# An encoder block on one core: the conditioning vector first, its later sums on two engines, and four changes of order

## The chip, the cores and the metric

The kernel runs as one program on one core of a Trainium2 chip. The core has TensorE (PE, matrix products; PEld is its loading of stationary operands), VectorE (DVE), ScalarE (ACT), GpSimd (POOL) and SyncE (SP), each with its own queue in program order, and 16 DMA engines that they share. SBUF holds the tiles, PSUM (eight banks of 128 x 512 float32) takes TensorE's results. The metric is the device time of one execution in microseconds; where several were run, their median.

## The reference, cut to what matters

One layer, 256 tokens of width 1024, all in float32. The conditioning vector c (1024) gives six modulation vectors of 1024 each: silu(c) times a matrix of 1024 x 6144, plus a bias.

```
mod = silu(c) @ w_ada + b_ada                       # 6 x 1024
h   = rmsnorm(x, g_pre_mix) * (1 + scale_m) + shift_m
proj = h @ w_in                                     # 5664 columns: q, k, v, z, xbc, dt
attn = mixture over 3 dilated windows (16 heads of 64, ALiBi)
y    = two-way SSD scan of conv5(xbc), dt = softplus(..), gated by silu(z), rmsnorm
x    = x + gate_m * rmsnorm(concat(attn, y) @ w_out, g_post_mix)
h   = rmsnorm(x, g_pre_ffn) * (1 + scale_f) + shift_f
logits = h @ w_router + b_router                    # top 4 of 32 experts, softmax over the 4
ffn = sum over experts e of weight_e * (swiglu(h @ w_gate_up[e] + b) @ w_down[e] + b)
x    = x + gate_f * rmsnorm(ffn, g_post_ffn)
```

All 32 experts' weights (12 MB each) are read. An expert gets only the tokens that chose it, gathered by a product with a selection matrix; up to 64 fit into the first pass, and a branch per expert (`more`) takes further passes where there are more.

## The kernel before, in words

**The ring of weights.** Every large weight comes through one list `loads` of tiles of 128 x 2048 float32 (1 MB). `consumed` (L133) marks tiles as used and issues the next loads on SyncE (L150), in list order, into whatever slots are free. The ring has 7 slots at first (`RING`); `more_ring` adds 3, 3, 2, 3 and 3 more as the mixer's pools close, 21 in the end. The list: eight chunks of w_ada for shift and scale of the mixer (`W_ADA`, 128 rows x 2048 columns each), then the 22 tiles of w_in (256 columns each) with 16 tiles of w_ada for the other four vectors (`W_MOD`) between them from the seventh on, then eight of w_out, then twelve for each expert (eight of gate and up, four of down). A DMA signals its landing on one of a few semaphores, taken in turn; a DMA whose semaphore is still owed by an earlier one waits in its queue. x, the small vectors, the identity and conv_w are issued on ScalarE's queue instead (L246 to L257), in program order with ScalarE's own work.

**Head.** The small vectors land as rows of one tile `vec` and are transposed into columns `colv` (L289, L290); silu of the first eight columns gives `csT`. x is squared and scaled into `xn` and transposed into four PSUM banks (L371). `ada_sums` (L330) multiplies each chunk by csT as stationary operand, four column groups side by side; `ada` transposes the result into columns `modT`. Then, for each of eight blocks of 128 channels, ScalarE writes the modulated block (L443), and it is cut into a rounded high part `hh` and the rest `hl`.

**Projections.** A float32 product is done as three products of high and low parts (`mm3`, L386). The weights are cut half a tile at a time by `split`: ScalarE makes the high part (L377), VectorE the low part (L378); `ahead` issues that two halves before their use, with three buffers. For each of the 22 tiles n and half h, `unit` issues 48 or 24 products, then `mod_half` (L355) the products of a quarter of the modulation: tile i = n - 5, two of its four blocks of rows, four column groups each, accumulated in PSUM; `cs31` holds column k of csT in the middle of zeros, so that group g's sum lands in its own row. `evac` takes results out, in pieces.

**Background pieces.** `bg` (L315) issues the next piece of a list of generators: `cumulate`, `ssd_bg`, then `att_bg` (L696). It is called in the middle of a unit and after it, as often as `PACE` says (four times a tile from n = 14 on). `att_bg` issues, for head pair j, when `ready` says that its keys are there: scores with VectorE's minimum and ScalarE's exponentials (`att_scores`), a piece; the scaling of pair j-1 (`att_norm`, L664); once the values are there, the product with the values of pair j-2, a piece; the transposes of pair j-1 (`att_T`, L678), a piece. `softplus_dt` (L469) is a chain on 128 x 64 elements in two pieces: the addition of the bias (L472), transposes on TensorE (L475) and exponentials at n = 1, first half; twenty small VectorE operations at n = 1, second half.

**Experts.** After the router, `rank` and `cnt` (the experts' counts) are made; `count(0)` (L1052) loads a count into a register of TensorE, ScalarE and VectorE, `hint` (L1055) tells each engine's branch prefetcher what the count makes of the branch; eight gathers follow (L1040, L1043), the softmax of the routing weights `comb` (L1066 to L1072), and the loop over experts, which begins with the branch (L1223). For the last expert the work goes in halves; `down_piece` (L1312) accumulates both column halves in one PSUM bank (partitions 0 to 63 and 64 to 127), which VectorE (L1338) and ScalarE (L1339) then copy out.

## Time and profile before

| | us |
|---|---|
| median of three runs | 1299.23 (1298.46 to 1304.69) |
| profiled execution: its own time, its span | 1302.06, 1300.0 |
| TensorE busy | 1166.8 (90%) |
| VectorE busy | 360.4 (28%) |
| ScalarE busy | 279.8 (22%) |
| GpSimd busy | 23.7 (2%) |
| DMA | 465.99 MB, mean 358 GB/s |
| mean granted clock of TensorE | 0.981 |

The strips of the page, 40 slices of 32.5 us each; a digit is the share in tenths, PEclk the granted clock in tenths of full speed:

```
PE   3799989988899999999989999999999999999986
PEld 1788867766333333333353333333333334333332
DVE  0686664457221111112211121111111121111112
ACT  1576556654111000001110011000000011100001
PEclk9899999999799999999999999999999899999998
DMA  8877655486699999999999999999999999999995
GB/s 312 259 250 258 207 184 178 157 315 263 268 415 414 412 415 412 416 413 415 415 405 406 413 415 413 414 414 414 415 415 404 415 410 415 404 413 408 416 345 205
```

The mixer fills the first ten slices, the experts the rest. Shares of busy time are means over these two stages with different limits. Where a row gives an idle time in brackets, the arrow names what ended it. In the table by stretches a number of instructions follows each engine's busy time.

### The profile page before, as it was taken

To read this page: it belongs to the slowest core of one execution; us is meant where nothing else is said; L and a number is where in the kernel's file an instruction comes from. 1 tells how busy PE (TensorE), PEld (TensorE's weight loads), DVE (VectorE), ACT (ScalarE), POOL (GpSimd) and SP (SyncE) were. 2 spreads that over 40 slices of the span, in tenths; PEclk is the share of its full clock that TensorE was granted. 3 is DMA by queue.
4 is the path that set the end of the run, shared out by engine and by line. 5 is a ranking of instruction groups with operands and counts; after the bars stand their busy time and mean duration, and the time that the engine had idled before them with its cause. 6 is when DMAs were issued, how large, how long until landed. Compare 5 with 4: busy or idle time off the path is not lost. (4 is left out here: it accounts for less than half of the span.)

```text
span 1300.0 us, 17236 instructions
## 1 busy us (share of the span) xinstructions
PE 1166.8 (90%) x6901; PEld 586.7 (45%) x6901; DVE 360.4 (28%) x768; ACT 279.8 (22%) x619; POOL 23.7 (2%) x34
## 2 busy tenths in 40 slices
PE   3799989988899999999989999999989999999986
PEld 1788867766333333333353333333333334333332
DVE  0686664457221111112211121111111121111112
ACT  1576556654111000001110011000000011100001
POOL 0100010010000000000000000000000000000000
PEclk9899999999799999999999999999999899999998
DMA  8877655486699999999999999999999999999995
GB/s 312 259 250 258 207 184 178 157 315 263 268 415 414 412 415 412 416 413 415 415 405 406 413 415 413 414 414 414 415 415 404 415 410 415 404 413 408 416 345 205
DMA packets 115645, 465.99 MB, mean 358 GB/s; under 512 B 11083, under 2 KB 34291, under 8 KB 82707
## 3 DMA queue, kind: packets, MB, share of 16 engines
q1 hardware_dynamic: 114752, 462.39, 90.2%
q8 instruction: 107, 1.75, 0.6%
q10 hardware_dynamic: 723, 1.33, 0.3%
q14 instruction: 63, 0.52, 0.1%
HBM read 462.65 MB, written 1.05 MB: 357 GB/s over the span
## 5 line engine op out<-in xcount | busy, mean ns | idle before, releaser
L1128 PE MATMUL pq_g<-w,xg 128*64 128x512 f32 x992 | 263.2, 598 | 2.8 <-DMA w<-in_w_gate_up_dram 2.8
L1128 PE MATMUL pq_u<-w,xg 128*64 128x512 f32 x992 | 263.2, 596 | 1.3 <-issue 1.3
L1166 PE MATMUL pq_u<-w,aT 128*64 128x512 f32 x992 | 219.7, 595 | 2.1
L1140 ACT ACTIVATE sg<-g 128x512 f32<-128x512 f32 (+1 forms) x32 | 19.9, 623 | 689.5 <-DVE g L1139 689.5
L1139 DVE TENSOR_SCALAR g<-pq_g 128x512 f32<-128x512 f32 (+1 forms) x32 | 21.9, 683 | 449.5 <-PE pq_g L1128 254.3
L1128 PEld LDWEIGHTS pq_u<-w,xg 128*64 128x64 f32 x992 | 75.0, 138 | 137.3 <-issue 135.2
L1128 PEld LDWEIGHTS pq_g<-w,xg 128*64 128x64 f32 x992 | 74.2, 138 | 130.3 <-issue 110.6
L1166 PEld LDWEIGHTS pq_u<-w,aT 128*64 128x64 f32 x992 | 68.5, 137 | 131.6 <-issue 120.2
L386 PE MATMUL ps_pj<-hh,wh 128*128 128x256 f32 x296 | 89.7, 303 | 3.4 <-DVE hh L444 3.4
L378 DVE TENSOR_TENSOR wl<-w,wh 128x1024 fp32r<-128x1024 f32 x60 | 74.7, 1246 | 58.7 <-ACT wh L377 58.6
L386 PE MATMUL ps_pj<-hh,wl 128*128 128x256 f32 x296 | 85.4, 288 | 2.3 <-DVE wl L378 2.3
L386 PE MATMUL ps_pj<-hl,wh 128*128 128x256 f32 x296 | 85.3, 288 | 0.0
L1230 DVE COPY y<-pq_u 128x512 f32<-128x512 f32 x31 | 21.4, 692 | 227.8 <-PE pq_u L1166 227.4
L1040 PEld LDWEIGHTS pq_m<-sel,xt 128*128 128x128 f32 x544 | 67.1, 201 | 26.3 <-issue 25.6
L1040 PE MATMUL pq_m<-sel,xt 128*128 128x128 f32 (+1 forms) x544 | 73.1, 291 | 1.2 <-DVE top L1066 1.2
L1043 ACT ACTIVATE xg<-pq_m,modT,g 128x128 f32<-128x128 f32 x128 | 48.3, 458 | 110.5 <-PE pq_m L1040 110.5
L377 ACT ACTIVATE wh<-w 128x1024 fp32r<-128x1024 f32 x60 | 63.5, 1058 | 28.7 <-PE ps_t L386 10.9
L386 PEld LDWEIGHTS ps_pj<-hh,wh 128*128 128x128 f32 x296 | 58.1, 196 | 9.3 <-issue 9.0
L1177 PE MATMUL o<-y,sT 64*128 64x512 f32 x248 | 61.6, 615 | 0.0
L386 PEld LDWEIGHTS ps_pj<-hh,wl 128*128 128x128 f32 x296 | 57.9, 196 | 2.8 <-DVE wl L378 2.7
L386 PEld LDWEIGHTS ps_pj<-hl,wh 128*128 128x128 f32 x296 | 58.0, 196 | 0.1
L1095 PE MATMUL pq_m<-kc,selw 128*128 128x128 f32 x66 | 16.3, 315 | 29.0 <-DVE selw L1091 28.2
(316 smaller groups left out, 1032.9 us busy)
## 6 DMA issues: line engine op xcount, KB each, us to landing
w<-in_w_gate_up_dram SPq DMA_DIRECT2D x248, 1024.0 KB, 19.2
w<-in_w_down_dram SPq DMA_DIRECT2D x127, 1024.0 KB, 20.0
w<-in_w_ada_dram SPq DMA_DIRECT2D x24, 1024.0 KB, 5.2
w<-in_w_in_dram SPq DMA_DIRECT2D x22, 1024.0 KB, 13.3
w<-in_w_out_dram SPq DMA_DIRECT2D x8, 1024.0 KB, 4.8
w<-in_w_gate_up_dram SPq DMA_DIRECT2D x16, 512.0 KB, 15.2
xt<-in_x_dram ACTq DMA_DIRECT2D x1, 1024.0 KB
w<-in_w_down_dram SPq DMA_DIRECT2D x2, 512.0 KB
```

Of the source, the lines that this page charges most:

```text
L377: act.activation(hi.bitcast(F32R), src, AF.Copy)
L378: dve.tensor_sub(lo.bitcast(F32R), src, hi)
L386: pe.matmul(out_ap, u, v, start=first and i == 0, stop=last and i == 2, skip_group_check=True)
L1040: pe.matmul(p[:, w * i:w * i + w], res[:, t, k * 128:(k + 1) * 128], sel[:, t], start=(t == 0), stop=(t == 1))
L1043: act.activation(xg[:, k], p[:, w * i:w * i + w], AF.Identity, bias=m_shift[:, k:k + 1], scale=g1[:, 8 + k:9 + k])
L1095: pe.transpose(p[:, 128 * t:128 * t + 128], selw[:, t].rearrange("p d c -> p (d c)"), ident)
L1128: pe.matmul(dst[cs * q:cs * q + cs, 0:w], xg[:, k], weight(k, o, w), start=False, stop=(k == KD - 1), tile_position=(0, cs * q), skip_grou ...
L1139: dve.tensor_scalar(g, pg, 7.0, None, op0=OP.min)
L1140: act.activation(s, g, AF.Sigmoid, scale=1.702)
L1166: pe.matmul(py[cs * q:cs * q + cs, 0:w], a4[:, k % nj, k // nj, :], weight(KD + k, w * q, w), start=(k == 0), stop=(k == KD - 1), tile_pos ...
L1177: pe.matmul(oacc[t][hf], sT[64 * q:64 * q + 64, 128 * t:128 * t + 128], y[64 * q:64 * q + 64, :], start=False, stop=False, tile_position=( ...
L1230: dve.tensor_copy(y, py)
```

## The change

The parts, in program order. (1) `c` is the first DMA on ScalarE's queue, then the identity, then x. Its eight columns are transposed and put through silu by themselves; the seven other vectors and conv_w are issued after silu. The squares and the scaling of x are emitted after the second chunk of `ada_sums`, the transposes of the other vectors (`columns`) and of x (`tokens_T`) after the sixth. (2) `mod_half`: of the two tiles of a group g, the first (rows 0 to 511 of w_ada) is multiplied and summed on VectorE into `macc` (one scaling, three multiply-adds of 128 x 512), the second stays on TensorE; `macc` is then summed over its partitions on TensorE with a column of ones (`one31`), four products more. (3) The first tile's split goes behind the first block of h; high parts of odd blocks are made on ScalarE, all low parts on VectorE. (4) `softplus_dt` has one piece more: the transposes come at n = 1, second half, the small operations at n = 2. (5) `att_bg` issues the scaling of pair j-1 ahead of the scores of pair j, and keys or values count as ready only two background steps after their copy. (6) The first branch's hint is a fixed one, emitted before the counts are made; the count is loaded after the gathers; two products on a bank nobody reads follow the clearing of the output banks. (7) The last expert's result goes into two banks, one for each column half, and the transposes of its second half are emitted ahead of all down products.

```diff
@@ -238,23 +238,29 @@
...
     dtc = mi.tile([32, 1], F32, name="dtc")
     arow = mi.tile([P, 32], F32, name="arow")
-    cs31 = mi.tile([P, KD, 63], F32, name="cs31")
+    one31 = mi.tile([P, 63], F32, name="one31")
+    pool.memset(one31, 0.0)
+    pool.memset(one31[:, 31:32], 1.0)
+    cs31 = mi.tile([P, 4, 63], F32, name="cs31")
     pool.memset(cs31, 0.0)
     dsk = mx.tile([P, 8], F32, name="dsk")
     wdt = cvb[:, 1, :].rearrange("p (k n) -> p k n", k=KD)
-    act.dma_start(xt, x[0].rearrange("(t p) d -> p t d", p=P))
     vo = {}
+    def vec_in(r, half, *items):
+        for nm, src, n in items:
+            act.dma_start(vec[r:r + n, half, :], src.rearrange("(n q) -> n q", q=128))
+            r += n
     r = 0
-    dve.memset(vec, 0.0)
-    for nm, src, n in (("c", c[0], 8), ("gpm", g_pre_mix[0], 8), ("bada", b_ada[0], 48),
-                       ("gpf", g_pre_ffn[0], 8), ("cb", conv_b[0], 12), ("gsn", g_ssd_norm[0], 8),
-                       ("gqm", g_post_mix[0], 8), ("gqf", g_post_ffn[0], 8)):
-        act.dma_start(vec[r:r + n, 0, :], src.rearrange("(n q) -> n q", q=128))
+    for nm, n in (("c", 8), ("gpm", 8), ("bada", 48), ("gpf", 8), ("cb", 12), ("gsn", 8), ("gqm", 8), ("gqf", 8)):
         vo[nm] = r
         r += n
+    vec_in(0, 0, ("c", c[0], 8))
     act.dma_start(ident, keep[:, 0:P])
-    act.dma_start(vec[0:60, 1, :], conv_w[0].rearrange("t (n q) -> (t n) q", q=128))
+    act.dma_start(xt, x[0].rearrange("(t p) d -> p t d", p=P))
     kb_f = flat_v[:, 1536:1536 + sum(KEEPB.values())]
     def loads_dt():
@@ -278,24 +284,37 @@
     def col(nm, j):
         return colv[:, vo[nm] + j:vo[nm] + j + 1]
-    for t in range(2):
-        act.activation(vt[:, t, :], xt[:, t, :], AF.Square, accum_out=tiny[:, t:t + 1])
-    for t in range(2):
-        rstd_of(tiny[:, 2 + t:3 + t], tiny[:, t:t + 1])
     xn = xtk
-    for t in range(2):
-        dve.tensor_scalar(xn[:, t, :], xt[:, t, :], tiny[:, 2 + t:3 + t], None, op0=OP.mult)
     pv = ps("t", 2)
-    pe.transpose(pv[:, 0:128], vec[:, 0, :], ident)
-    pe.transpose(pv[:, 128:188], vec[0:60, 1, :], ident[0:60, 0:60])
-    dve.tensor_copy(colv[:, 0:108], pv[:, 0:108])
-    dve.tensor_copy(colv[:, 108:168], pv[:, 128:188])
-    ghalf = mx.tile([P, KD], F32, name="ghalf")
-    dve.tensor_scalar(ghalf, colv[:, vo["gsn"]:vo["gsn"] + 8], 0.5, None, op0=OP.mult)
+    pe.transpose(pv[:, 64:72], vec[0:8, 0, :], ident[0:8, 0:8])
+    dve.tensor_copy(colv[:, 0:8], pv[:, 64:72])
     csT = mx.tile([P, KD], F32, name="csT")
     act.activation(csT, colv[:, 0:8], AF.Silu)
-    dve.tensor_copy(cs31[:, :, 31:32], csT[:, :, None])
-    dve.tensor_copy(ident_b, ident)
+    vec_in(8, 0, ("gpm", g_pre_mix[0], 8), ("bada", b_ada[0], 48))
+    act.dma_start(vec[0:60, 1, :], conv_w[0].rearrange("t (n q) -> (t n) q", q=128))
+    vec_in(60, 1, ("gpf", g_pre_ffn[0], 8), ("cb", conv_b[0], 12), ("gsn", g_ssd_norm[0], 8),
+           ("gqm", g_post_mix[0], 8), ("gqf", g_post_ffn[0], 8))
+    def tokens_in():
+        dve.tensor_copy(cs31[:, :, 31:32], csT[:, 4:8, None])
+        for t in range(2):
+            act.activation(vt[:, t, :], xt[:, t, :], AF.Square, accum_out=tiny[:, t:t + 1])
+        for t in range(2):
+            rstd_of(tiny[:, 2 + t:3 + t], tiny[:, t:t + 1])
+        for t in range(2):
+            dve.tensor_scalar(xn[:, t, :], xt[:, t, :], tiny[:, 2 + t:3 + t], None, op0=OP.mult)
+    ghalf = mx.tile([P, KD], F32, name="ghalf")
+    def columns():
+        pe.transpose(pv[:, 0:64], vec[0:64, 0, :], ident[0:64, 0:64])
+        dve.tensor_copy(colv[:, 8:64], pv[:, 8:64])
+        pe.transpose(pv[:, 128:232], vec[0:104, 1, :], ident[0:104, 0:104])
+        dve.tensor_copy(colv[:, 64:108], pv[:, 188:232])
+        dve.tensor_copy(colv[:, 108:168], pv[:, 128:188])
+        dve.tensor_scalar(ghalf, colv[:, vo["gsn"]:vo["gsn"] + 8], 0.5, None, op0=OP.mult)
+        dve.tensor_copy(ident_b, ident)
     def bias_parts(pl):
@@ -311,9 +330,11 @@
     pssq = mp.tile([P, 512], F32, name="pssq", tag="ssq", bufs=1)
     bg_list = []
+    ticks = [0]
     def bg(n=1):
         for _ in range(n):
+            ticks[0] += 1
             while bg_list:
                 try:
...
@@ -337,8 +358,12 @@
...
             if k == 1:
                 loads_dt()
+                tokens_in()
             if k == 3:
                 loads_cum()
+            if k == 5:
+                columns()
+                tokens_T()
         loads_late()
         return pa
@@ -352,23 +377,42 @@
                        pt.rearrange("p (j q r) -> p q j r", j=4, q=4)[:, :, :, 0],
                        colv[:, vo["bada"]:vo["bada"] + 16].rearrange("p (q j) -> p q j", q=4))
+    def mod_sums(g, lhs, w, first=False):
+        for b in range(4):
+            pe.matmul(pssq[32 * b:32 * b + 32, 128:256], lhs, w[:, 128 * b:128 * b + 128],
+                      start=first, stop=True, tile_position=(0, 32 * b), skip_group_check=True)
     def mod_half(i, a):
         w = wt[W_MOD[i]].rearrange("p (k n) -> p k n", k=4)
         g = i // 2
+        if i % 2 == 0 and a == 0:
+            macc[g] = mb.tile([P, 512], F32, name="macc", tag="macc", bufs=1)
         for kk in range(2 * a, 2 * a + 2):
-            k = 4 * (i % 2) + kk
-            for b in range(4):
-                pe.matmul(pssq[32 * b:32 * b + 32, 128:256], cs31[:, k, 31 - g:63 - g], w[:, kk, 128 * b:128 * b + 128],
-                          start=(i == 0 and k == 0), stop=True, tile_position=(0, 32 * b), skip_group_check=True)
+            if i % 2:
+                if kk == 2:
+                    mod_sums(g, one31[:, 31 - g:63 - g], macc.pop(g))
+                mod_sums(g, cs31[:, kk, 31 - g:63 - g], w[:, kk, :], kk == 0 and g == 0)
+            elif kk == 0:
+                dve.tensor_scalar(macc[g], w[:, kk, :], csT[:, 0:1], None, op0=OP.mult)
+            else:
+                dve.scalar_tensor_tensor(macc[g], w[:, kk, :], csT[:, kk:kk + 1], macc[g], op0=OP.mult, op1=OP.add)
         if a:
             consumed(W_MOD[i] + 1)
-    ptx = [ps("bc", 2), ps("bc", 2), ps("pj", 3), ps("pj", 3)]
-    for k in range(KD):
-        for t in range(2):
-            o = (k % 2) * 256 + t * 128
-            pe.transpose(ptx[k // 2][:, o:o + 128], xn[:, t, k * 128:(k + 1) * 128], ident)
+    macc = {}
+    ptx = []
+    def tokens_T():
+        ptx.extend([ps("bc", 2), ps("bc", 2), ps("pj", 3), ps("pj", 3)])
+        for k in range(KD):
+            for t in range(2):
+                o = (k % 2) * 256 + t * 128
+                pe.transpose(ptx[k // 2][:, o:o + 128], xn[:, t, k * 128:(k + 1) * 128], ident)
     def split(i, a, pl=None, bufs=3):
@@ -436,13 +480,17 @@
...
     dve.scalar_tensor_tensor(g1[:, 0:8], modT[:, 8:16], 1.0, colv[:, vo["gpm"]:vo["gpm"] + 8],
                              op0=OP.add, op1=OP.mult)
-    ahead(0)
     for k in range(KD):
         src = ptx[k // 2][:, (k % 2) * 256:(k % 2) * 256 + 256]
         full = big("hfull")[:, 0:S]
         act.activation(full, src, AF.Identity, bias=modT[:, k:k + 1], scale=g1[:, k:k + 1])
-        dve.tensor_copy(hh[:, k, :], full)
-        (pool if k % 2 else dve).tensor_sub(hl[:, k, :], full, hh_[:, k, :])
+        if k % 2:
+            act.activation(hh[:, k, :], full, AF.Copy)
+        else:
+            dve.tensor_copy(hh[:, k, :], full)
+        dve.tensor_sub(hl[:, k, :], full, hh_[:, k, :])
+        if k == 0:
+            ahead(0)
     ahead(1)
@@ -470,6 +518,7 @@
         ut = flat_v[0:32, 0:S]
         dve.tensor_scalar(ut, pdt[0:32, 0:S], dtc, None, op0=OP.add)
+        yield
         pt = ps("t", 2)
         for t in range(2):
...
@@ -664,7 +713,11 @@
                 act.activation(sc[:, t, :], sc[:, t, :], AF.Copy, scale=st[:, 6 + t:7 + t])
     prTs, done_in = {}, []
-    ready = {"k": 0, "v": 0}
+    ready = {"k": [], "v": []}
+    def is_ready(what, i):
+        return len(ready[what]) > i and ticks[0] > ready[what][i] + 1
     def att_T(j):
         pr = pts.pop(j)
@@ -695,15 +748,15 @@
     def att_bg():
         for j in range(HEADS // 2 + 2):
+            if 0 < j < 9:
+                att_norm(j - 1)
             if j < 8:
-                while ready["k"] <= j // 2:
+                while not is_ready("k", j // 2):
                     yield
                 att_scores(j)
                 yield
-            if 0 < j < 9:
-                att_norm(j - 1)
             if j > 1:
-                while ready["v"] <= (j - 2) // 2:
+                while not is_ready("v", (j - 2) // 2):
                     yield
                 att_out(j - 2)
...
@@ -736,13 +789,13 @@
...
             act.activation(vt[:, :, c0 - 2048:c0 - 1792], v3, AF.Copy)
             yield
-            ready["v"] += 1
+            ready["v"].append(ticks[0])
         elif c0 >= 1024:
             j = (c0 - 1024) // 128
...
                 kT[j + i] = blk("k")
                 act.activation(kT[j + i], v3[:, i], AF.Copy)
-            ready["k"] += 1
+            ready["k"].append(ticks[0])
             yield
         else:
...
@@ -776,7 +829,7 @@
...
                 chain = softplus_dt(pdt)
                 next(chain)
-            if n == 1 and h:
+            if (n, h) in ((1, 1), (2, 0)):
                 next(chain, None)
             pace = PACE[0 if n < 8 else 1 if n < 14 else 2][2 * h:]
...
@@ -1002,6 +1055,8 @@
         return mq.tile([P, 512], F32, name="pq_" + tag, tag=tag, bufs=bufs)
+    tc.mark_branch_hint_location("more0", hint="LikelyTaken", engines=[ET.PE, ET.Activation, ET.DVE])
     rank = mo.tile([P, 2, NE], F32, name="rank")
     cnt = mo.tile([1, NE], I32, name="cnt")
...
@@ -1019,6 +1074,7 @@
...
     pe.matmul(pcn, ones_b, mask_b[:, 1, :], start=False, stop=True)
     clear(1)
+    keep_warm(pq("u", 1), 2)
     dve.scalar_tensor_tensor(rank, mask, -FAR, prk[:, 0:2, :], op0=OP.mult, op1=OP.add)
     dve.tensor_copy(cnt, pcn[0:1])
@@ -1054,10 +1110,9 @@
     def hint(e, n):
         tc.mark_branch_hint_location(f"more{e}", hint=(n > C), engines=engines)
-    n = count(0)
-    hint(0, n)
     for ks in HALF:
         gather(sel_n, xgs[0], ks)
+    n = count(0)
     comb = mo.tile([P, 2, NE], F32, name="comb")
@@ -1313,7 +1368,7 @@
...
             o = 256 * f + 128 * (k % 2) + C * (k % 4 // 2)
             for q in range(2):
-                pe.matmul(py[C * q:C * q + C, :], aT[:, o:o + C], weight(KD + k, 512 * q, 512),
+                pe.matmul(py[q][C * q:C * q + C, :], aT[:, o:o + C], weight(KD + k, 512 * q, 512),
                           start=(k == 0), stop=(k == KD - 1), tile_position=(0, C * q), skip_group_check=True)
     gate_up_half(0, range(KD))
@@ -1323,10 +1378,9 @@
...
     gate_up_half(1, range(4, KD))
     glu_half(1)
-    py = pq("m", 2)
-    down_piece(0, (0, 1))
+    py = pq("g", 1), pq("u", 1)
     turn_half(1)
-    down_piece(0, (2, 3))
+    down_piece(0, range(4))
     down_piece(1, range(4))
@@ -1335,8 +1389,8 @@
     fo = [[spare[0][:, 1024 * t + 512 * i:1024 * t + 512 * i + 512] for i in range(2)] for t in range(2)]
     y2 = mo.tile([P, 512], F32, name="y2", tag="g")
-    dve.tensor_copy(y[0:C], py[0:C])
-    act.activation(y2[C:P], py[C:P], AF.Copy)
+    dve.tensor_copy(y[0:C], py[0][0:C])
+    act.activation(y2[C:P], py[1][C:P], AF.Copy)
     rsf = []
     for t in range(2):
```

## Rows read from the trace of the kernel before

**Rows 1.** Stretches: length; busy PE, PEld, DVE, ACT, POOL; clock; DMA share; GB/s
```profile
346.00:1278.00 932.00, 861.59 (x4410) 344.10 (x4406) 155.87 (x324) 93.57 (x238) 1.90 (x1) 0.99 1.01 409
340.51:347.34 6.83, 5.36 (x16) 1.80 (x18) 1.74 (x9) 1.56 (x2) 0.00 (x0) 0.50 0.01 4
```

**Rows 2.** SyncE's timeline from 318 us: start, length, engine, line, operation, count
```profile
328.74 18.14 SPq L150 DMA_DIRECT2D w<-in_w_down_dram  x2
```

**Rows 3.** The table by stretches, two stretches of the projections
```profile
84.00:100.00 16.00, 15.59 (x178) 13.76 (x174) 15.41 (x31) 10.29 (x18) 0.00 (x0) 1.00 0.78 248
100.00:181.00 81.00, 80.56 (x872) 69.50 (x870) 53.45 (x88) 49.97 (x107) 6.71 (x7) 1.00 0.69 225
```

**Rows 4.** The timeline of the start; in brackets idle time before it
```profile
0.74 26.33 SPq L150 DMA_DIRECT2D w<-in_w_ada_dram  x8
21.19 1.97 PE L371 MATMUL ps_bc<-kc,xtk 128*128 128x128 f32 x8
24.79 8.04 PE L335 MATMUL ps_pj<-w,csT 128*32 128x512 f32 x64
37.57 0.55 PE L386 MATMUL ps_pj<-hh,wh 128*128 128x256 f32 x1 [3.36 <-DVE hh L444]
```

**Rows 5.** The table by stretches, two stretches of the start
```profile
10.00:15.00 5.00, 0.00 (x0) 0.00 (x0) 0.00 (x0) 1.98 (x2) 0.00 (x0) 1.00 0.62 201
25.00:30.00 5.00, 5.00 (x44) 1.23 (x40) 0.00 (x0) 0.00 (x0) 0.00 (x0) 1.00 0.54 164
```

**Rows 6.** The waits of SyncE's queue: who for whom, us, times, longest
```profile
SPq L150 <- DMA cvb<-in_c_dram: 9.4, 1, 9.4
```

**Rows 7.** The DMA issues: tile, queue, count, size, us to landing
```profile
cvb<-in_conv_w_dram ACTq DMA_DIRECT2D x1, 30.0 KB, 8.6
```

**Rows 8.** The timeline of TensorE, from 44 us
```profile
51.78 0.31 PE L475 MATMUL ps_t<-kc,vt 32*128 32x32 f32 x2 [2.67 <-DVE vt L472]
```

**Rows 9.** The timeline of TensorE, from 83 us
```profile
83.86 0.64 PE L362 MATMUL pssq<-w,cs 128*32 128x128 f32 x16
84.44 0.39 PE L386 MATMUL ps_pj<-hh,wh 128*128 128x256 f32 x1
```

**Rows 10.** The tile xtk's instructions: ns least, median, most, when, forms
```profile
L912 DVE SCALAR_TENSOR_TENSOR xt<-xtk,tiny,xt x4: 747/750/753, 318.9 to 323.9; 128x512 f32<-128x512 f32 x4
L287 DVE TENSOR_SCALAR xtk<-xt,tiny x2: 752/752/753, 16.6 to 17.8; 128x1024 f32<-128x1024 f32 x2
```

**Rows 11.** TensorE's waits from 180 to 262 us, and the timeline of the longest
```profile
PE ps_t L678 <- ACT sc L664: 7.3, 3, 4.1
...
193.30 2.15 PE L678 MATMUL ps_t<-kc,sc 128*128 128x128 f32 x8 [4.12 <-ACT sc L664]
```

**Rows 12.** The timeline of ScalarE, from 180 us
```profile
186.99 1.04 ACT L377 ACTIVATE wh<-w 128x1024 fp32r<-128x1024 f32 x1
...
192.76 1.69 ACT L664 ACTIVATE sc<-sc,st 128x256 f32<-128x256 f32 x4
```

**Rows 13.** The table by stretches, around two falls of the clock
```profile
193.74:197.15 3.41, 3.41 (x16) 3.33 (x17) 0.08 (x1) 2.85 (x5) 0.00 (x0) 0.50 0.00 0
197.15:200.56 3.41, 3.41 (x41) 3.08 (x40) 1.14 (x1) 1.41 (x3) 0.00 (x0) 1.00 0.31 52
...
241.52:244.94 3.42, 3.42 (x17) 3.19 (x17) 0.70 (x2) 2.86 (x6) 0.00 (x0) 0.50 0.00 0
```

**Rows 14.** The timeline of TensorE, around the first expert
```profile
332.28 6.11 PE L1040 MATMUL pq_m<-sel,xt 128*128 128x128 f32 x32 [1.21 <-DVE top L1066]
...
341.98 0.64 PE L1124 MATMUL pq_g<-bias,kb 96*64 96x512 bf16 x2 [3.60 <-DVEq L1223]
```

**Rows 15.** The table by stretches, around the gathers
```profile
330.27:337.10 6.83, 5.62 (x26) 4.86 (x23) 1.39 (x7) 1.04 (x3) 0.00 (x0) 0.50 1.00 414
```

**Rows 16.** The timeline of the end, the last result's two copies
```profile
1288.02 0.68 DVE L1338 COPY y<-pq_m 64x512 f32<-64x512 f32 x1 [4.71 <-PE pq_m L1316]
...
1288.80 0.59 ACT L1339 ACTIVATE y<-pq_m 64x512 f32<-64x512 f32 x1 [5.81 <-DVE y L1338]
```

## The prediction

> **What bounds the kernel now.** I read the page's strip of slices first: the DMA digits are 9 from the eleventh slice nearly to the last, so most of the span is a stream of weights. The table by stretches makes it exact: from 346 to 1278 us the DMA engines are busy 1.01 of the time at 409 GB/s, while TensorE has 70 us to spare; just before, from 340.5 to 347.3, they move 4 GB/s [rows 1]. Why they stand still is in SyncE's timeline: of a pair of issues begun at 328.74 the second ends at 346.88 [rows 2]. All 21 ring tiles are full, and the next load waits until expert 0 has used its first tile. From there 363 of the 384 expert tiles of 1.05 MB are still to come: 381 MB in 932 us is 408 GB/s. So the end is the time of expert 0's first release, plus a fixed stream, plus the tail after 1278. A microsecond saved before 346 is one saved at the end, whichever engine saves it; one saved between 346 and 1278 is worth nothing. Before 346 TensorE is nearly always busy (80.56 of 81 us from 100 to 181, [rows 3]), so the terms below are its work and its waits.
>
> **Head.** The modulation sums run from 24.79 to 32.83 and the first projection follows at 37.57 [rows 4]. What lies between (copy, four transposes, gains, then high and low half of the first tile) stays: the split of that tile now stands behind the first normed block on ScalarE instead of ahead, but the third product of the first unit still waits for the low half. Odd blocks' rounding goes to ScalarE and GpSimd's subtractions to VectorE; TensorE waits for neither. So the head moves by the end of the sums. That end was set by the eighth chunk, which needs a freed slot: SyncE is through with the eighth issue only at 27.07 [rows 4]. DMA lost 1.9 us in 10 to 15 us ((1-0.62)x5) and 2.3 in 25 to 30 ((1-0.54)x5) [rows 5]. With c first, its silu no longer waits for x and all the vectors, so chunks are used as they land, slots come free in time, and the second pause goes: 2.3. The first has another cause: SyncE's third chunk waited 9.4 us for the landing of c [rows 6], because transfers take turns on few landing semaphores. Eight small loads now come after x on ScalarE's queue, so some chunk will wait for them again; I keep that pause. Against the gain: the 16 token transposes (eight took 1.97 [rows 4], so 3.9) and two column transposes (at the same price 0.5) now sit on TensorE between the sixth and the seventh chunk, ahead of two chunks of 1.0 (8.04/8). The sixth lands two tiles (5.1 us at 409 GB/s) before the last, so 4.4+1.0 ends 0.3 late, more if the clock is lower by then. I take 1.5. Upper bound 4.2, both pauses gone. Lower bound: ScalarE, which issues the small loads in order, is held until the sixth chunk has landed; then come two squares (priced like the scalings of the same size, 0.75 each [rows 10]), two scalings, 0.8 of small steps (estimate), 4.4 of transposes and two chunks, 10.2 in all, where 6.1 (5.1 and one chunk) was the pace of the loads: 4.1 late, so 2.3-4.1, about -2.
>
> The eight loads are the risk: conv_w, issued beside weight chunks, needed 8.6 us to land [rows 7]. The Trainium skill, "DMA: Bandwidth & Descriptors", section "Queues, rings and completion order", says that each DMA engine takes turns between the queues' rings by packets and serves one ring in order. By that c comes in at once between the first chunk's packets, but the small loads stand behind x in ScalarE's ring, and any chunk that must wait for one of them comes after x; the trace's 8.6 us agrees. By that rule the head tends to its lower end, a rival below.
>
> **Softplus.** TensorE waited 2.67 us for VectorE's addition before transposing it [rows 8]. The transposes move one half tile back; in between stand 24 products, and the long rest of the chain moves half a tile too, past a tile's low half. 2.5 saved. Bounds 0 (VectorE, now with the long rest at another place, is late for a low half by as much) and 2.67.
>
> **Modulation sums.** One half (16 matmuls) runs from 83.86 to 84.44, 0.58 [rows 9]; there are 32. Sixteen go, 9.3; eight of the others get half as many again, 2.3. Net 7.0 of a TensorE that has nothing free there [rows 3]. VectorE gets eight groups of one scaling and three multiply-adds of 128x512: the multiply-add of this form took 0.75, a scaling of twice the columns 0.75 [rows 10], so between 0.38 and 0.75; I take 0.45, near half. 2.7 a group, 21.6 in all, in order with the low halves that TensorE needs. From 100 to 181 VectorE has 27 us free; but from 84 to 100 it is busy 15.41 of 16 [rows 3], so the first group comes up to 2 late. I take 1.6 off: 5.4. Bounds 7.0 and -14.6 (all 21.6 felt).
>
> **Attention.** TensorE waits three times from 180 to 262, 7.3 us, for the normalised probabilities before transposing them, the longest from 189.18 to 193.30 [rows 11]. They were scaled from 192.76, in 1.69, behind the next pair's four exponentials. Now the scaling stands ahead of those: ScalarE is through with a split at 188.03 [rows 12], so it ends near 189.7, half a microsecond after TensorE asks. The two others were 1.6 each and go. 6.7 saved. Behind two of these waits the clock was granted at half for 3.4 us: 16 and 17 matmuls against 41 [rows 13], so 2.1 and 2.0 lost; without the waits I count 3.0 of the 4.1. The added wait (a step's distance from key or value to use) holds nothing up: attention is issued piecewise, two key tiles take 6 of 8 pieces; the last pair slips a piece or two into the output projection, where the pieces have room. Sum 9.7. Bounds 3 (half the waits stay, and the clock with them) and 11.4 (7.3+4.1).
>
> **Start of the experts.** The gathers start at 332.28 after 1.21 idle, which registers' loading ahead of them explains in part; moved behind, with two warming matmuls in the gap, so of 0 to 1.2 I take 0.5. The 3.60 before expert 0 stays [rows 14]: it is VectorE's branch, behind the softmax, behind ScalarE's eight evictions; the register load on ScalarE may add 0.5 there. A fixed hint instead of a computed one removes an operation on each engine and nothing that is waited for. The clock is at half from 330.27 to 337.10 [rows 15]; if the warming ends that sooner, the gathers (6.11) shorten by up to 2.5. I take 1.0; bounds -0.5 and 3.5.
>
> **Tail.** ScalarE's copy of the last result starts at 1288.80, when VectorE's of 0.68 is over [rows 16], though both could start at 1288.0; two banks part them: 0.6 (0 to 0.8). The transposes go ahead of the down products instead of between, the same sum.
>
> **Sum.** 1.5+2.5+5.4+9.7+1.0+0.6 = 20.7. The profiled execution took 1302.06 for its span of 1300.0, so 1281.4; it lies 2.8 above the median of 1299.23, so 1278.6.
>
> **Rivals.**
> - The attention wait moves: TensorE stands at the scores or at the values instead, the clock falls as before. For: ScalarE keeps all its work. Against: a half tile of 24 products lies between each piece and the next. 3 instead of 9.7: 1285. Chance 0.13.
> - The late loads hold the head: ScalarE's squares wait behind its own issues, -2 instead of 1.5 and the first VectorE group late: 1282. For: [rows 6, 7]. Chance 0.12.
> - The head gains both pauses and the gathers run at full clock: 4.2 and 3.5 for 1.5 and 1.0, so 1272 to 1273. Against: [rows 6]. Chance 0.10.
> - The front becomes bound by its loads, so that nothing arrives earlier: 1299. Against: DMA stands idle before 346 [rows 1]. Chance 0.04.
> - Slower: VectorE becomes the bound from 84 to 262. Each added operation delays a low half that TensorE waits for: -14.6 for 5.4, and the reciprocals and reductions of attention come late too, so its 9.7 go: 20.7-20-9.7 = -9, 1308. It decides once VectorE is busy over 0.95 there; it was 0.66 from 100 to 181 and would be 0.8. Chance 0.03.
>
> **How the numbers follow.** The forecast has 0.58. All upper ends together save 29.6, 1270, and single runs of this kernel lie up to a few us apart, so the range begins at 1266; it goes to 1289, where half of the 20.7 is left. It takes in the first three rivals and leaves out the last two. 0.5% is 6.5 us, about what a measurement can tell. Faster: all but the last two, 0.93; same 0.04; slower 0.03.
>
> **What would show it.** Sums ending near 31 and the first projection near 36; no wait before the softplus transposes; 320 modulation matmuls for 512, VectorE near 0.8 and no new wait for low halves; the probabilities' transposes without idle time and the clock full from 190 to 250; expert 0's first release near 326, then a stream of the same 932 us. Wrong it would be if that release came earlier and the end did not, or if TensorE waited for VectorE between 84 and 262.

## The result and the profile after

The changed kernel took 1285.56 us (median of four runs, 1284.73 to 1289.18) against 1299.49 (four runs, 1298.46 to 1304.69): a ratio of 0.989, 95% interval 0.9857 to 0.9923. Run again beside three experiments it took 1285.21 (1284.32 to 1286.21) against 1301.54 (eleven runs, 1298.31 to 1304.01): 0.988, 0.9863 to 0.9897. The forecast of 1278.6 (1266 to 1289) has the sign and holds the time in its range, but lies 7 us below it. Between the two profiled executions, 1302.06 and 1284.73, 17.3 of the forecast 20.7 came. The medians differ by 13.9 in the first comparison and by 16.3 in the second: the kernel before spreads over 6 us, and its first runs were low ones.

The page's strips of the changed kernel, 40 slices of 32.1 us:

```profile
PE   5889989889799999999989999899988999989986
DVE  1788866666111112111112111111112021111113
PEclk8999989989899999999999999999999899999999
DMA  9878745758799999999999999999999999999995
```

PE's first ten digits are hardly fuller than before, and the ninth PEclk digit (257 to 289 us) is an 8 (the first, sixth and eleventh are taken up below). The table by stretches answers [rows 1]:

```profile
330.00:1262.00 932.00, 859.22 (x4410) 343.76 (x4406) 155.55 (x324) 93.58 (x238) 1.90 (x1) 0.99 1.01 409
322.86:329.69 6.83, 3.71 (x12) 1.38 (x14) 1.74 (x9) 1.34 (x2) 0.00 (x0) 0.50 0.01 4
```

The stream is the same 932 us at 409 GB/s, and just ahead of it the DMA engines still stand at 4 GB/s. SyncE's first issue after the full ring moved from 346.50 to 330.18, and the span from 1300.0 to 1282.9: 16.3 at the start of the stream and 0.7 behind it make the whole. So the frame of the prediction holds, and the question is what happened before 330.

To see that, take the 1272 products of the helper `mm3` (projections and output projection). They are the same in all kernels, so the start of the n-th can be compared. Each mark is that start in us; n = 0 is the first projection, 768 lies where attention begins, 1104 near the end of attention, 1176 to 1200 in the output projection. Behind them come the start of the gathers and of expert 0, and the stream's first issue.

```
n            0     48     96    384    768   1104   1176   1200  gather expert0 stream   span
before     37.57  46.10  54.98 100.58 176.25 274.02 295.25 303.32 332.28 341.98 346.50 1300.0
after      33.82  43.72  49.74  96.49 168.04 253.06 275.99 288.62 316.50 325.98 330.18 1282.9
gained      3.75   2.38   5.24   4.09   8.21  20.97  19.26  14.69  15.78  15.99  16.32   17.1
```

At n = 1104 a little more than the whole forecast of 20.7 had been saved, though 1.6 of that forecast (start of the experts, tail) was still to come. 6.3 of it was lost again between 1104 and 1200, in the output projection. There the timelines show first VectorE, then TensorE, then SyncE's issues of the changed kernel:

```profile
269.12 1.23 DVE L422 TENSOR_TENSOR wl<-w,wh 128x1024 fp32r<-128x1024 f32 x1 [1.05 <-ACT wh L421]
276.37 0.42 DVE L329 CAST bias<-bgu 96x512 bf16<-96x512 f32 x1 [6.02 <-DMA bgu<-in_b_gate_up_dram]
...
279.05 1.20 DVE L422 TENSOR_TENSOR wl<-w,wh 128x1024 fp32r<-128x1024 f32 x1
```

```profile
280.31 0.80 PE L430 MATMUL ps_bc<-wl,blk_q 128*128 128x512 f32 x1 [3.93 <-DVE wl L422]
```

```profile
261.41 3.09 SPq L150 DMA_DIRECT2D w<-in_w_gate_up_dram  x4
266.77 1.25 SPq L324 DMA_DIRECT2D bgu<-in_b_gate_up_dram  x3
```

Read from the end: TensorE stood 3.93 us for a low half `wl`. VectorE made it late because ahead of it, in program order, is the third piece of the experts' gate-and-up bias (`bias_parts`, four pieces of 96x512, loaded through one tile `bgu`), and that piece stood 6.02 us for its load. The load was issued at 266.77, behind four weight tiles of 1 MB that SyncE had issued at 261.41. Then the clock fell:

```profile
278.49:285.32 6.83, 5.01 (x12) 3.81 (x12) 4.90 (x9) 0.00 (x0) 0.00 (x0) 0.50 0.11 29
```

In the kernel before, the third piece waited 1.45 us, and TensorE stood for nothing behind it. Its one wait there, 2.31, is for a low half behind the fourth piece (1.77), and the clock did not fall (timelines of VectorE, TensorE and SyncE, kernel before):

```profile
291.06 0.42 DVE L310 CAST bias<-bgu 96x512 bf16<-96x512 f32 x1 [1.45 <-DMA bgu<-in_b_gate_up_dram]
...
296.72 0.42 DVE L310 CAST bias<-bgu 96x512 bf16<-96x512 f32 x1 [1.77 <-DMA bgu<-in_b_gate_up_dram]
...
300.67 0.50 PE L386 MATMUL ps_bc<-wl,blk_q 128*128 128x512 f32 x1 [2.31 <-DVE wl L378]
...
277.57 3.40 SPq L150 DMA_DIRECT2D w<-in_w_gate_up_dram  x4
286.05 1.26 SPq L305 DMA_DIRECT2D bgu<-in_b_gate_up_dram  x3
```

Four weight tiles stand ahead of the third load there too, but the load was issued 8.5 us behind the first of them; in the changed kernel it was 5.4.

### The profile page after: what moved, and what is told of

Its sections match the earlier page's. It is cut to its first block, busy times and chain, and to the rows that moved or that the text cites. A ratio compares the mean times of both kernels' runs of the same rounds, so it can differ in the third digit from the quotient of the medians.

```text
span 1282.9 us, 16887 instructions
## 1 busy us (share of the span) xinstructions
PE 1155.6 (90%) x6712; PEld 577.5 (45%) x6712; DVE 379.7 (30%) x801; ACT 277.8 (22%) x622; POOL 19.8 (2%) x32
## 5 line engine op out<-in xcount | busy, mean ns | idle before, releaser
L1183 PE MATMUL pq_u<-w,xg 128*64 128x512 f32 x992 | 260.3, 595 | 2.2 <-issue 2.2
L1183 PE MATMUL pq_g<-w,xg 128*64 128x512 f32 x992 | 260.4, 596 | 2.1 <-DMA w<-in_w_gate_up_dram 2.1
L1179 PE MATMUL pq_g<-bias,kb 96*64 96x512 bf16 (+1 forms) x66 | 13.1, 400 | 32.9 <-DVE y L1285 26.3
```

The source lines that it names most:

```text
L1179: pe.matmul(dst[cs * q:cs * q + cs, 0:w], kbv["e3"][0:3 * NE, e:e + 1].to_broadcast([3 * NE, cs]), bias3[:, o:o + w], start=True, stop=Fal ...
L1183: pe.matmul(dst[cs * q:cs * q + cs, 0:w], xg[:, k], weight(k, o, w), start=False, stop=(k == KD - 1), tile_position=(0, cs * q), skip_grou ...
```

## Experiments

My theory (theory 1): everything before the stream adds up, and what is missing was lost at the bias load. Rivals: (2) the front is by now held by its loads or by VectorE, so that a wait taken away only moves; (3, later 4) the sums given to VectorE cost what they save. Each kernel was timed 4 to 12 times. Each group of four shared a chip and its runs of before: bias_once, no_sums, no_att and no_head with a median of before of 1302.79; the changed kernel again, before_att, bias_act and no_soft with 1301.54; the other four with 1301.98. The differences in the text are of the medians as they stand. By the ratios, those across groups come out up to 1.3 us otherwise (no_att 14.4 for 15.7, sums_early 5.2 for 4.3).

| kernel | median, us | ratio to before, 95% interval |
|---|---|---|
| changed kernel, again | 1285.21 | 0.988, 0.9863 to 0.9897 |
| bias_once | 1275.73 | 0.9805, 0.9785 to 0.9826 |
| no_sums | 1283.59 | 0.9861, 0.9841 to 0.9881 |
| no_att | 1300.88 | 0.9991, 0.9977 to 1.0005 |
| no_head | 1283.83 | 0.9862, 0.9842 to 0.9881 |
| before_att | 1290.13 | 0.9914, 0.9895 to 0.9933 |
| bias_act | 1289.85 | 0.9912, 0.9897 to 0.9926 |
| no_soft | 1288.18 | 0.9898, 0.9881 to 0.9916 |
| bias_spread | 1279.62 | 0.9836, 0.9813 to 0.9858 |
| sums_early | 1280.94 | 0.984, 0.9819 to 0.986 |
| both | 1275.21 | 0.980, 0.9779 to 0.9821 |
| no_delay | 1285.94 | 0.9881, 0.9858 to 0.9905 |

Their marks, from one profiled execution each:

```
n              0     48     96    384    768   1104   1176   1200  gather expert0 stream
after        33.82  43.72  49.74  96.49 168.04 253.06 275.99 288.62 316.50 325.98 330.18
after_again  33.29  43.20  49.22  95.98 167.53 252.53 275.47 287.50 315.38 325.00 329.51
bias_once    34.64  44.55  50.56  97.35 168.87 253.87 276.79 282.23 310.12 317.71 321.70
no_sums      33.26  43.18  49.20  95.85 171.51 253.19 276.12 287.38 315.25 322.86 326.94
no_att       34.28  44.17  50.20  96.98 168.51 272.31 293.51 304.84 332.72 342.32 346.84
no_head      36.89  45.22  51.23  97.98 169.52 254.53 276.71 289.42 317.29 324.89 328.77
before_att   37.29  45.62  55.82 101.38 177.04 258.70 280.92 292.30 321.33 330.35 334.87
bias_act     33.41  43.33  49.42  96.17 167.70 252.69 284.76 292.90 320.77 330.21 334.28
no_soft      35.66  45.60  56.94 102.87 174.39 259.40 282.32 294.08 321.95 331.26 335.11
bias_spread  33.55  43.48  49.57  96.38 167.92 253.48 275.94 281.38 310.75 320.21 324.72
sums_early   33.48  43.39  49.41  96.18 168.26 249.91 272.83 285.49 313.37 320.97 325.49
both         33.69  43.59  49.60  96.36 168.47 250.11 273.02 278.46 308.25 316.52 320.55
no_delay     33.46  43.38  49.39  96.16 167.70 256.86 278.08 289.01 316.91 326.20 330.02
```

One thing runs through the table: in bias_once, no_sums, no_head, sums_early and both, the wait between the gathers and expert 0 is 1.9 us shorter than in the changed kernel, which none of their edits aimed at (see the end). Their medians hold these 1.9 us; the marks up to the gathers do not.

**The changed kernel again.**

> The changed kernel once more, beside the others on one chip and with a second trace. If the wait at the output projection is a matter of the loads' order (theory 1), the 3.9 us before the low half and a fall of the clock behind it are there again, and the median is 1284.5 to 1287. If it was a matter of that one execution (rival), the wait is under 2 and the first release earlier by as much, and the trace of the first run told nothing. The start of expert 0 has taken 3.6 us in three of five traces and 5.5 in two (this kernel's own among them): if that differs from execution to execution and not from kernel to kernel, either may be seen.

As theory 1 had it: from n = 1176 to 1200 it took 12.0 us (12.6 in the first trace), with 3.3 us of waiting for the first low half, and the clock at half for 3.4 us from 278.93. The wait belongs to the kernel.

**bias_once: three of the four bias loads and their waits away.**

```diff
-            b = pl.tile([3 * NE, 512], F32, name="bgu", tag="bgu")
-            for i in range(3):
-                sp.dma_start(b[NE * i:NE * i + NE, :], b_gate_up[0, :, o:o + 512])
+            if o == 0:
+                b = pl.tile([3 * NE, 512], F32, name="bgu", tag="bgu")
+                for i in range(3):
+                    sp.dma_start(b[NE * i:NE * i + NE, :], b_gate_up[0, :, o:o + 512])
```

> The changed kernel, with the experts' gate-and-up bias loaded once (the first 512 columns) and that tile used for all four pieces; VectorE's work on them stays, the three later loads and the waits for them go (the other bias columns are not read). Theory 1 (the time is the first expert's release plus a fixed stream; a part of the gain was lost at the output projection, where VectorE stood 6.0 us for a bias load issued at 266.8 behind four weight tiles of 1 MB, TensorE 3.9 us for VectorE's low half, and the clock then fell to half for 6.8 us): the wait of 3.9 at 276.4 and the half clock from 278.5 go, against 1 or 2 us that may return; first release 4.5 to 7.5 us earlier than 330.2, and the median about 1285.6-6 = 1280. Theory 2 (the whole front is by now held by its loads or by VectorE, so that a wait taken away shows up at the next place): first release less than 1.5 earlier, median 1284 to 1286.

9.5 us faster than the changed kernel's 1285.21 (9.8 than its first median), more than theory 1 asked. From 1176 to 1200 it took 5.44 us, 7.2 less than the changed kernel and 2.6 less than the kernel before, and nothing of this came back at a later mark. Rival 2 falls. The rest lies at the start of expert 0, 7.6 from the gathers' start for 9.5, which this edit does not touch (the 1.9 named above).

**bias_act: the bias loads from ScalarE's queue.**

```diff
-                sp.dma_start(b[NE * i:NE * i + NE, :], b_gate_up[0, :, o:o + 512])
+                act.dma_start(b[NE * i:NE * i + NE, :], b_gate_up[0, :, o:o + 512])
```

> The changed kernel with the loads of the experts' bias issued on ScalarE's queue instead of SyncE's; nothing is left out. Theory 1 (the bias stands behind four weight tiles in SyncE's ring): from its own queue the third piece lands within 5 us of its issue instead of 9.6, the wait of 3.9 falls under 1 and the clock stays up: 1277 to 1281. Rival (the loads share landing semaphores or the DMA engines' time, whichever queue they come from): they land as late as before, or ScalarE is held at the issue and its high halves are late: 1283 to 1288.

My remedy was wrong, for the reason that the rival named. In ScalarE's timeline the issue waits until VectorE has freed `bgu`, and ScalarE's own high halves stand behind it; the two longest of TensorE's waits from 250 to 290 us follow.

```profile
257.96 1.26 ACTq L324 DMA_DIRECT2D bgu<-in_b_gate_up_dram  x3
259.27 1.06 ACT L421 ACTIVATE wh<-w 128x1024 fp32r<-128x1024 f32 x1 [4.46 <-issue]
...
282.28 1.26 ACTq L324 DMA_DIRECT2D bgu<-in_b_gate_up_dram  x3
283.65 2.95 ACT L421 ACTIVATE wh<-w 128x1024 fp32r<-128x1024 f32 x3 [8.27 <-issue]
```

```profile
PE ps_t L742 <- ACT prT L733: 3.5, 1, 3.5
PE ps_bc L430 <- ACT wh L421: 3.4, 1, 3.4
```

"issue" stands where the profile sees no releaser: the issue ahead in the queue is what held it. The third piece was used 7.5 us after its issue began (272.00 to 279.49), against 9.6 from SyncE's queue; but it was issued 6.6 us behind the four tiles here and 5.4 there, so whether the queue or the shared engines set this stays open.

**bias_spread: the same loads, VectorE's work on them placed later.**

```diff
-        if k in (1, 3, 5, 6):
-            next(bias_job, None)
+        for _ in range({1: 2, 3: 2, 7: 1}.get(k, 0)):
+            next(bias_job)
...
+        if k == 0:
+            next(bias_job)
     ahead(M0 + 7)
+    for _ in range(2):
+        next(bias_job, None)
```

(the piece has a `yield` more in its middle.)

> The changed kernel with VectorE's work on the third and fourth pieces of the experts' bias placed later, each in two parts: the third behind the low halves of the seventh and of the first step of the second half, the fourth behind the last low half; the loads stay on SyncE's queue, nothing is left out. Theory 1 (what costs is that a low half stands behind a bias piece whose load is late): the wait of 3.3 to 3.9 us near 276 and the fall of the clock behind it go, without ScalarE being held; output projection some 28.5 long instead of 35, median 1277 to 1281. Rival (VectorE has no room for the 5.4 us of the two pieces later either): waits for low halves between 282 and 295 or for the sums of the projection take their place, 1283 to 1286.

As theory 1 had it, with nothing left out: 5.44 us from 1176 to 1200, the clock whole there, median 1279.62. TensorE's waits from 262 to 300 us, all of them:

```profile
PE ps_pj L975 <- DVE xt L971: 1.4, 1, 1.4
```

That one is the rival's small share: the fourth piece now stands ahead of the sums of the projection, and 1.5 is lost between 1200 and the gathers.

**no_att and before_att: the attention's order undone, and alone.** The first puts the scaling back behind the scores and drops the distance; the second makes that part of the change, and nothing else, in the kernel before.

```diff
-            if 0 < j < 9:
-                att_norm(j - 1)
             if j < 8:
                 while not is_ready("k", j // 2):
                     yield
                 att_scores(j)
                 yield
+            if 0 < j < 9:
+                att_norm(j - 1)
```

> The changed kernel with the attention's order of before: scores of pair j ahead of the scaling of pair j-1, keys and values ready at once. Theory 1: the three waits for the scaled probabilities (7.3 us before) and at least one fall of the clock between 185 and 250 come back, 8 to 11 us up to 262; at the output projection the bias load then comes in time, 2 to 4.6 us back: 4 to 8 us later, 1289.5 to 1293.5. Theory 2: under 2 us later.

> The kernel before with the attention's new order alone (scaling of pair j-1 ahead of the scores of pair j, keys and values ready two steps later). If its price is its own (the three waits of 7.3 us and the clock behind two of them, 8 to 11 us up to 262, less 1.7 that slip into the output projection and 1 to 3 for the bias load there): 5 to 8 us faster than before, 1295 to 1298. If its price depends on the other parts (undone in the changed kernel it cost 15 us, with waits of 2.6, 3.0 and 3.0 and four falls of the clock): the same as here alone or less, and the 15 come from VectorE's added work in the old order. If it is worth 15 by itself: 1287 to 1288.

Both missed by being too small. Undone, it costs 15.7 us (1300.88 against 1285.21): nearly all of what the changed kernel gains. From n = 768 to 1104 the changed kernel takes 85.0 us and this one 103.8. TensorE's waits from 180 to 262 us there, of 0.9 us and more:

```profile
PE ps_t L731 <- ACT sc L713: 8.6, 3, 3.0
PE ps_pj L430 <- ACT vt L790: 1.1, 1, 1.1
```

Against it the changed kernel, the same stretch:

```profile
PE ps_pj L430 <- DVE blk_k L746: 1.6, 1, 1.6
PE ps_t L731 <- DVE blk_k L746: 1.3, 2, 0.8
```

The waits for the scaled probabilities `sc` are gone. 2.9 us for `blk_k`, the low part that VectorE makes of a pair's result, stand in their place, which neither no_att nor the kernel before has. With the old order the clock was at half for 17.1 us of that stretch (from 181.22, 188.05, 211.94 and 239.25), in the changed kernel for 6.8 (from 179.50). Alone in the kernel before, it makes 81.7 us of 97.8 in that stretch, 16.1 saved, and the clock from 181 to 262 is 1.00; the median falls by 11.4. It then loses 4.3 from 1104 to 1200 (33.6 for 29.3), with a bias wait of 4.77 us on VectorE. But the wait does not come with this part alone: no_att, which has the old order, waits 3.15.

**no_delay: the order kept, the distance of two steps away.**

```diff
-        return len(ready[what]) > i and ticks[0] > ready[what][i] + 1
+        return len(ready[what]) > i
```

> The changed kernel without the distance of two background steps between a key's or value's copy and its use; the new order of scaling and scores stays. If the distance does nothing (as the prediction had it): 1284.5 to 1286, and the same row of waits. If it is what takes the 15 us of the attention part: waits for the keys' and values' copies on ScalarE appear between 180 and 262, and it is more than 3 us slower.

1285.94, the same time. The distance is not without effect: without it TensorE waits again for copies on ScalarE, and n = 1104 comes 3.8 later, but 1.7 of that is back by n = 1176 and 1.7 more by 1200, where VectorE's bias wait is 2.83 us instead of 6.02; the difference is then 0.4. So most of the 18.8 us up to n = 1104 is the order's, 14.6 (103.8 to 89.2 from n = 768), and 4.1 the distance's. Whether these 4.1 would show in the time of a kernel without the bias wait was not tried. The longest of TensorE's waits from 180 to 262 us:

```profile
PE ps_t L731 <- ACT prT L733: 1.7, 2, 1.0
PE ps_pj L430 <- ACT vt L790: 1.6, 1, 1.6
PE ps_bc L688 <- ACT blk_k L797: 1.6, 3, 0.9
```

**no_sums and sums_early: the shared modulation sums undone, and only where VectorE has room.** no_sums takes the old `mod_half`. sums_early shares the first five groups and leaves three to TensorE:

```diff
-        if i % 2 == 0 and a == 0:
+        if i % 2 == 0 and a == 0 and g < 5:
...
-            if i % 2:
+            if g > 4:
+                mod_sums(g, cs31[:, 4 * (i % 2) + kk, 31 - g:63 - g], w[:, kk, :])
+            elif i % 2:
```

> The changed kernel with the modulation sums all on TensorE again (512 products for 320, nothing on VectorE). Theory 1: TensorE gets back 192 products of 0.036 us, 6.9 us, and the waits for low halves at 74.8 to 84.9 (3.6 us together) stay, since VectorE's first product of the sums starts only at 84.8; the bias load comes in time again where TensorE is later, so 1.5 of the 3.9 at the output projection goes: 4 to 7 us later, 1290 to 1292.5. Theory 3 (the sums on VectorE cost what they save, which is why less came than was forecast): the waits of 74 to 85 go with them, and the time is 1284.5 to 1287.5.

> The changed kernel with the modulation sums shared with VectorE only for the first five of the eight groups (up to about 165 us, ahead of the attention); the last three are all on TensorE as before. Theory 4 (the shared sums gain 0.86 us a group while VectorE has room, and lose it again under the attention's chains, where no_sums had none of the waits of 1.45, 1.2, 0.7 and 1.6 us for VectorE): 4 us gained at 168 us stay, the waits near 170, 177 and 241 go, and the output projection begins 1.5 to 4 us earlier than in the changed kernel: median 1281.5 to 1284. Rival (the waits belong to the front's being early, not to VectorE's sums): they stay, three groups' products of 2.6 us come on top: 1286 to 1289.

no_sums was meant to tell 4 to 7 us from none, and it shows none: 1283.59, lower than the changed kernel's median by 1.6 us, about the 1.9 that come from the start of expert 0. The marks say where they went. Up to n = 768 the shared sums are worth 4.1 us (no_sums goes from 0.64 ahead at 384 to 3.47 behind), 0.8 a group as counted. By 1104 only 0.8 is left. The price stands around 170 us, VectorE and then TensorE of the changed kernel:

```profile
168.43 0.48 DVE L399 TENSOR_SCALAR macc<-w,csT 128x512 f32<-128x512 f32 x1
168.94 0.75 DVE L401 SCALAR_TENSOR_TENSOR macc<-w,csT,macc 128x512 f32<-128x512 f32 x1
...
170.92 0.69 DVE L622 TENSOR_TENSOR ee<-ee,cbm 128x512 f32<-128x512 f32 x1
...
174.44 2.04 DVE L401 SCALAR_TENSOR_TENSOR macc<-w,csT,macc 128x512 f32<-128x512 f32 x2
```

```profile
171.75 1.05 PE L630 MATMUL ps_t<-ee,xtk 128*64 128x256 f32 x6 [1.45 <-DVE ee L622]
178.33 0.70 PE L688 MATMUL ps_bc<-blk_k,blk_q 64*128 64x256 f32 x2 [1.23 <-DVE st L700]
```

1.2 us of sums stand ahead of a short chain of the scan (`ee`) that TensorE uses next, and 2.0 more ahead of the scores' minimum. Behind these waits the clock fell for 6.8 us, at 179.50. In no_sums and sums_early the waits of 1.45 and 1.23 are absent and the clock is whole from 100 to 270. sums_early is worth 3.1 us at n = 1104, as theory 4 had it; of its median's 4.3 (1280.94), 1.9 is the start of expert 0. Its rival, that these waits come from the front's being early, falls also by no_soft, which reaches n = 768 6.4 later than the changed kernel and has waits of 1.44 and 1.23 there.

**both: bias_spread and sums_early together.**

> Both edits at once: the bias pieces placed later, the shared sums in five groups only. Theory 1 and 4 together: 6 to 10 us faster than the changed kernel, 1275 to 1279. If the two meet the same wait: no faster than the better of the two alone.

1275.21, at the lower end of what was expected, and the two add up: at n = 1200, where the start of expert 0 has no part yet, 7.2 and 3.1 us alone and 10.2 together. The medians, 5.6 and 4.3 under the changed kernel's 1285.21 alone and 10.0 together, add up as well, but 1.9 of the 4.3 and of the 10.0 is the start of expert 0. It beats both kernels of this case.

**no_head: the head of before.** The edits of parts 1 and 3 are undone: x first and all vectors in one tile, squares and transposes ahead of the sums, the first split ahead of the normed blocks.

> The changed kernel with the head of before (c after x, all vectors in one tile, x's squares and transposes ahead of the modulation sums, first split ahead of the normed blocks, GpSimd's subtractions). Theory 1 with VectorE as the bound from 59 to 92 us: the first projection starts 3 to 4 us later (37 to 37.6), but the waits for low halves between 74 and 85 (3.6 us) shrink by 2 to 3, so that the end is only 0.5 to 2 us later, 1286 to 1287.6. Without that bound: 3.7 later, 1289.3. If the head gained nothing that lasts: the same within 0.5.

At n = 0 it is 3.1 behind the changed kernel, at n = 48 1.5, and this 1.5 stays until 1104. So the head is worth 1.5 by these two executions (the new head's eleven traces reach n = 48 between 43.18 and 45.60, eight of them before 43.8, so that it can be off by about 1), and the waits between 74 and 87 us for split weights do not swallow it, against the expectation (they are 3.6 us in both). The median, 1283.83, is lower than the changed kernel's all the same: its start of expert 0 took 7.6 for 9.5.

**no_soft: softplus in two pieces.**

```diff
-        yield
...
-            if (n, h) in ((1, 1), (2, 0)):
+            if n == 1 and h:
```

> The changed kernel with softplus in two pieces as before (transposes at n = 1, first half, the small operations at n = 1, second half). The wait of 2.7 us ahead of the transposes comes back near 47 us. If nothing binds behind it: 2.7 later at 60 us and at the end, 1288. If VectorE is the bound from 59 to 92 us (theory 1): the waits for low halves at 74 to 85 (3.6 us) shrink in turn and the end is 0 to 1.5 later, 1285.5 to 1287.

TensorE's timeline of this kernel has both waits that the kernel before had near there:

```profile
51.31 0.42 PE L523 MATMUL ps_t<-kc,vt 32*128 32x32 f32 x2 [2.67 <-DVE vt L520]
...
68.00 0.39 PE L430 MATMUL ps_pj<-hh,wl 128*128 128x256 f32 x1 [1.74 <-DVE wl L422]
```

Behind the first, the clock was at half for 6.8 us, from 50.95. From n = 48 to 96 it lost 5.3; of what the two waits took, 4.5 is left at 384 and at 768. The median is 3.0 later. In the kernel before the same wait of 2.67 had no fall of the clock behind it. The head of this execution was 1.8 late by itself, with the same instructions up to there.

## Why the prediction was right or wrong

**The frame** held: a fixed stream from the first issue (953.5 us to the end before, 952.8 after, 952.0 to 954.5 in all fourteen traces), so that savings ahead of it carry one for one within about 1.5 us. Its check, "that release came earlier and the end did not", did not occur. What failed in "expert 0's first release near 326" (330.18) is the sum.

**Head, 1.5:** 1.5 by no_head, as forecast, though only in part by its reasons. The second pause of the loads went, as forecast (DMA was busy 1.01 of 25 to 30 us), and the sums ended at 30.43. But the first projection came at 33.82, not "near 36": what lies between did not stay, and TensorE's wait just ahead of the projection fell from 3.36 [rows 4] to 2.01, now for the high half of the first tile. Of the 3.75 so gained 1.4 went in the first unit. The first pause of the loads stayed, as the prediction kept it: in SyncE's waits the fourth chunk stood 11.9 us for b_ada, and DMA was busy 0.64 of 10 to 15 us.

```profile
SPq L150 <- DMA cvb<-in_b_ada_dram: 11.9, 1, 11.9
```

What the prediction took from the Trainium skill ("DMA: Bandwidth & Descriptors", "Queues, rings and completion order") agrees so far: b_ada, issued behind x on ScalarE's queue, landed at 13.95, only after x, whose last packet ended at 13.18. But the head did not go to its lower end for it.

**Softplus, 2.5:** right within about a microsecond against the kernel before: from n = 48 to 384 the changed kernel gains 1.7 on it. Undone it costs more, 3.0 by the medians and 4.5 by the marks, because of the fall of the clock in no_soft: from n = 64 to 112 that kernel loses 5.6 on the changed one, the kernel before 2.7. What the bound of 2.67 left out is that moving the long chain also takes away the next wait for a low half (1.92 in the kernel before, at 65.83). About 2.8 came back between 67.7 and 96.5 us of the changed kernel, where TensorE stands four times for split weights (3.6 us from 74.8 to 84.9) and VectorE is busy 0.87 of the time.

**Modulation sums, 5.4:** this step failed. Its prices were right (VectorE's sums 3.9 + 18.5 = 22.4 us for 21.6; TensorE's 14.0 for 20.6 us of busy time). The whole-kernel lines of these operations:

```profile
L401 DVE SCALAR_TENSOR_TENSOR macc<-w,csT,macc 128x512 f32<-128x512 f32 x24 | 18.5, 770 | 0.6
L383 PE MATMUL pssq<-w,cs 128*32 128x128 f32 x256 | 10.6, 285 | 0.0
L399 DVE TENSOR_SCALAR macc<-w,csT 128x512 f32<-128x512 f32 x8 | 3.9, 482 | 0.0
L383 PE MATMUL pssq<-macc,one 128*32 128x128 f32 x64 | 3.4, 285 | 0.0
```

What was wrong is "From 100 to 181 VectorE has 27 us free": an average over two kinds of work. The table by stretches of the changed kernel, against [rows 3]:

```profile
84.00:100.00 16.00, 14.72 (x148) 13.85 (x149) 15.60 (x29) 10.41 (x18) 0.00 (x0) 1.00 0.81 265
100.00:181.00 81.00, 77.27 (x768) 66.92 (x767) 67.21 (x116) 50.67 (x114) 7.43 (x8) 0.99 0.74 239
```

VectorE is at 0.83, as forecast, and no low half waits for the sums; yet TensorE lost 3.3 us that it didn't lose before, all of it after 168, where VectorE's operations come in short chains that TensorE uses at once. So the prediction's other sign of being wrong, "if TensorE waited for VectorE between 84 and 262", did occur (1.45, 1.23 and 1.61 us, where the kernel before has none over 0.7), with VectorE well under the 0.95 that the last rival named for it. I watched the low halves and priced the loss where VectorE is fullest (84 to 100), not where an answer is wanted soonest.

**Attention, 9.7:** the mechanism was right, the size wrong: 16.1 alone and 18.8 undone up to n = 1104, 11.4 and 15.7 in the time. [rows 11] and the term end at 262 us. In the kernel before, waits of 1.14, 1.15, 1.00 and 1.00 us of the last two pairs follow between 260 and 274, and they went too. The first rival, that the wait moves within attention, occurred only in small part: in before_att 0.8 us for `sc` and 1.2 for `blk_k` stand where the kernel before has 7.3 and 1.1.

**The output projection, nothing:** the missing term. "The last pair slips a piece or two into the output projection, where the pieces have room" had the slip (1.7 from 1104 to 1176) and not what else waits there. VectorE comes for the third piece 3.6 us after its load's issue in both kernels, but the load is used 9.6 us after its issue instead of 5.0, and the wait grows from 1.45 to 6.02 us. It cost 4.6 (12.63 for 8.07). In the traces this goes with how closely the load follows the first of the four tiles: issued 8.5 us behind it (before, no_att, no_delay) the wait is 1.5 to 3.2, issued 5.4 behind it (the changed kernel twice, before_att, no_sums, no_head, no_soft, sums_early) it is 4.7 to 6.0. It does not go with how early the front is: at n = 1104 no_att is 1.7 ahead of the kernel before and waits 3.15, no_delay is 17.2 ahead and waits 2.83. What sets the distance was not tried. By the rule of the fourth rival ("the front becomes bound by its loads") it is a small piece of that rival, which I gave 0.04: not the weights were late, but 192 KB of bias behind them.

**Start of the experts, 1.0:** 1.3 from n = 1200 to expert 0. The gathers took 4.01 us for 6.11 [rows 14], at full clock, and begin 0.1 after the warming; 1.9 of that went again in a longer wait ahead of expert 0:

```profile
316.50 4.01 PE L1096 MATMUL pq_m<-sel,xt 128*128 128x128 f32 x32
...
325.98 0.64 PE L1179 MATMUL pq_g<-bias,kb 96*64 96x512 bf16 x2 [5.47 <-DVE sel L1086]
```

**Tail, 0.6:** 0.6, from VectorE's copy to the end 11.97 us before and 11.33 after. The two copies of the last result start together, against [rows 16]:

```profile
1271.61 0.68 DVE L1392 COPY y<-pq_g 64x512 f32<-64x512 f32 x1 [7.71 <-PE pq_u L1371]
...
1271.70 0.59 ACT L1393 ACTIVATE y<-pq_u 64x512 f32<-64x512 f32 x1 [8.13 <-PE pq_u L1371]
```

By the marks the 17.1 us are: head 2.4 (up to n = 48), softplus and what came back of it 1.7 (to 384), sums 4.1 (to 768), then 12.8 (to 1104: 16.1 for attention as it is alone, less 3.3 for the sums' price), -1.7 (to 1176), -4.6 (to 1200), 1.3 (to expert 0), 0.3 (to the stream) and 0.7 behind it. So the total came near the forecast by errors of both signs: attention 6 to 9 too small, the sums about 5 too large, and a loss of 4.6 that was not there. That it lies in the range is in good part luck.
